# First modulation: half of its weight blocks through TensorE in float32, the other half on VectorE, and the scaled input split in two steps

## The chip, the core and the metric

The kernel runs on one core of a Trainium2 chip. The core has a matrix engine (TensorE, in the profile PE for matmuls and PEld for weight loads), three other compute engines (VectorE: DVE; ScalarE: ACT; GpSimd: POOL), an engine that issues the DMAs here (SyncE: SP), and 16 DMA engines that bring data from HBM into the on-chip memory (SBUF). Matmul results go to a second on-chip memory (PSUM), of 8 banks with 512 float32 columns on 128 partitions. The metric is the device time of one execution in microseconds; lower is better.

## The reference, cut to what matters

Six network stages run one after the other on a sequence of 512 tokens of width 1024. The change is at the very front of the first. There a condition vector `c` of 1024 numbers gives, by a matrix product with `w_ada`, a scale and a shift for each of the 1024 features:

```python
cond = jax.nn.silu(c)
mod = cond @ w_ada[l] + b_ada[l]                    # (1024) @ (1024 x 6144)
sh_m, sc_m, g_m, sh_f, sc_f, g_f = jnp.split(mod[:, None, :], 6, axis=-1)
h = layer_norm(x) * (1.0 + sc_m) + sh_m             # 512 x 1024
mix = hybrid_mixer(h, w_in[l], ...)                 # starts with h @ w_in
```

In the kernel `1 + sc_m` is G and `sh_m` is B; each needs 1024 x 1024 numbers of `w_ada`. Everything later waits for `h`.

## The kernel before, in words

Nearly all matmuls are float32 products built of three products in a reduced format: each operand is split into a high part (`hh`, `wh`) and the rest (`hl`, `wl`), and `mm3` (L116 to L120) issues high x high, low x high and high x low. A weight block is loaded by SP into one of five `wr` buffers, rounded into `wh` by ScalarE (L101), and the rest `wl` is taken by VectorE (L102). The first user of `h` is `dt_project` (a block of 48 columns), then come the projections of `proj_in`, each of 128 columns.

The head of the kernel is this. `cond_cols` makes `silu(c)` as a 128 x 8 tile: column k holds the 128 values of feature block k. `mix_load` loads X and normalises it (L306, L772, `rsqrt`, L776). `gemv_cols` runs twice, for G and for B. Each run has two halves of 512 columns, and each half four loads of 512 KB, 16 loads in all, numbered 1 to 16 here: 1 to 4 for G's first half, 5 to 8 for its second, 9 to 12 and 13 to 16 for B. A load brings two weight blocks of 128 x 512, one for an even k, `r[:, 0]`, and one for an odd k, `r[:, 1]`.

Every block is multiplied by its `cond` column, one number for each partition, and added up. The even blocks go through VectorE into `acc[0]` (L200, L202). The odd ones go into `acc[1]`: GpSimd multiplies the first (L200), ScalarE scales the second and third in place (L204) and GpSimd adds them (L205), and VectorE adds the last (L202). Then TensorE sums over the 128 partitions: each 128-column slice of an `acc` is the stationary operand and a column of ones the moving one (L209, eight float32 matmuls for a half, of which the trace shows two records each). VectorE takes the four columns from PSUM into G or B (L211). All four halves write into one PSUM tile, `sums`, one bank.

`mix_hT` transposes X on TensorE (L787), into four tiles of the pool `pa` and four of `pb`. For each of the eight feature blocks ScalarE then forms `h = X*G + B` (L791) and its high part (L792), and VectorE the low part (L793). One `pb` tile is `sums`, so the eighth block's transposes wait until another `pb` tile is free.

The program's text doesn't set the order of the instructions: a scheduler places them, each engine runs its list strictly in that order, and semaphores carry the waits between engines. A `wr` buffer is loaded anew when all that read it are done.

Of the kernel before, what the change touches and what calls it, by code (L numbers as in the profile page):

```python
# [7 lines left out]
F32 = mybir.dt.float32  # L8
F32R = mybir.dt.float32r
I32 = mybir.dt.int32  # L10
AF = mybir.ActivationFunctionType
OP = mybir.AluOpType
# [6 lines left out]
KD = 8  # L19
# [14 lines left out]
def blk(c):  # L34
    return slice(128 * c, 128 * c + 128)


class Kern:
# [148 lines left out]
    def gemv_cols(self, cond, w, n0, bcol, add, dst, p):  # L187


        nc = self.nc  # L190
        for h in range(2):
            c0 = n0 + 512 * h
            acc = [self.t(), self.t()]
            for k2 in range(4):
                r = self.wrp.tile([128, 2, 512], F32, name="wr", tag="wr")
                nc.sync.dma_start(r, w[k2 * 256:k2 * 256 + 256, c0:c0 + 512].rearrange("(k p) n -> p k n", p=128))
                for j, eng in enumerate((nc.vector, nc.gpsimd)):
                    k = 2 * k2 + j
                    if k2 == 0:
                        eng.tensor_scalar(acc[j], r[:, j], cond[:, k:k + 1], None, op0=OP.mult)  # L200
                    elif j == 0 or k2 == 3:
                        nc.vector.scalar_tensor_tensor(acc[j], r[:, j], cond[:, k:k + 1], acc[j], op0=OP.mult, op1=OP.add)  # L202
                    else:
                        nc.scalar.activation(r[:, j], r[:, j], AF.Copy, scale=cond[:, k:k + 1])  # L204
                        eng.tensor_add(acc[j], acc[j], r[:, j])  # L205
            cs = slice(4 * h, 4 * h + 4)
            for j in range(4):
                for i in range(2):
                    nc.tensor.matmul(p[:, 4 * h + j:4 * h + j + 1], acc[i][:, blk(j)], self.ones[:, 0:1],  # L209
                                     start=(i == 0), stop=(i == 1))  # L210
            nc.vector.scalar_tensor_tensor(dst[:, cs], p[:, cs], add, bcol[:, cs], op0=OP.add, op1=OP.add)  # L211

    def gemv(self, ends, cond, w, bcol, n0, kind, dst, scale=1.0, bias=0.0):
# [565 lines left out]
    def mix_hT(self, X, G, B):  # L779

        nc = self.nc
        self.new_hT()
        P = []
        for k in range(KD):
            p = self.pa() if k < 4 else self.pb()
            for t in range(NT):
                nc.tensor.transpose(p[:, blk(t)], X[:, t, blk(k)], self.ident)  # L787
            P.append(p)
        for k in range(KD):
            h = self.t()  # L790
            nc.scalar.activation(h, P[k], AF.Identity, bias=B[:, k:k + 1], scale=G[:, k:k + 1])  # L791
            nc.scalar.activation(self.hh[:, k], h, AF.Copy)  # L792
            nc.vector.tensor_sub(self.hl[:, k], h, self.hh[:, k].bitcast(F32))  # L793

    def mix_cols(self, V4):
        io, V = self.io, self.nc.vector
# [1641 lines left out]
```

## Time and profile before

| | us |
|---|---|
| median of 3 runs | 2830.43 (2826.44 to 2836.71) |
| the profiled execution's own time | 2836.87 |
| span, from its first to its last instruction | 2835.1 |
| TensorE busy | 2543.7, 90% of the span |
| VectorE, ScalarE, GpSimd busy | 1940.3, 1289.9, 757.9 |
| first projection's first matmul (L118) | at 44.61 |

All rows come from one execution. A timeline row has the start, the time from the start of the first to the end of the last instruction of the row, engine, line, operation, tile written <- tiles read, shapes, count, and in brackets how long the engine had been idle and what ended that. Ends of matmuls are modelled, so the distance between two starts is the better measure of a matmul. A float32 matmul has two records.

### The profile page before, as it was taken

The page shows a single profiled execution, that of the slowest core. Times are in us where ns is not written, and L with a number is a line of the kernel's source. Part 1 is how long each engine was busy: PE and PEld are TensorE (multiplying, and loading weights), DVE is VectorE, ACT ScalarE, POOL GpSimd, SP SyncE. Part 2 cuts the span into 40 slices and gives each one's busy share as a digit, 9 for nine tenths or more (in the row PEclk, how much of TensorE's full clock was granted, in tenths as well). Part 3 has the DMA queues.
Part 4 walks back from the last instruction along what each step waited for, and adds up shares of the span by engine and source line. Part 5 has one row for each costly group of instructions (what it writes and reads, how often), then busy time and mean ns, then how long its engine had stood idle before and what let it go on. Part 6 is the DMA issues. An engine that isn't in the chain of part 4 may idle for free.

```text
span 2835.1 us, 35075 instructions
## 1 busy us (share of the span) xinstructions
PE 2543.7 (90%) x12272; PEld 2072.8 (73%) x12272; DVE 1940.3 (68%) x3253; ACT 1289.9 (45%) x2138; POOL 757.9 (27%) x597
## 2 busy tenths in 40 slices
PE   6889899799999998798995898889999889899997
PEld 5777687578878776676774676767777777788885
DVE  7667678665667657679998877777767676843436
ACT  3444455533555433467774544453333435432412
POOL 2224333420122220321213213325345422500002
PEclk8999999899999897899997988999999989999998
DMA  7333244334454674689986243234444556433331
GB/s 224 87 92 99 74 119 117 85 87 126 142 172 139 197 246 145 217 279 341 362 311 160 82 127 114 77 116 130 138 140 129 159 198 197 123 108 97 97 97 60
DMA packets 382014, 425.95 MB, mean 150 GB/s; under 512 B 35447, under 2 KB 249578, under 8 KB 381834
## 3 DMA queue, kind: packets, MB, share of 16 engines
q1 hardware_dynamic: 375322, 401.11, 45.6%
q0 software_dynamic: 5936, 20.48, 2.3%
q8 instruction: 97, 1.59, 0.2%
q10 hardware_dynamic: 576, 2.10, 0.2%
q14 instruction: 83, 0.68, 0.1%
HBM read 389.14 MB, written 32.11 MB: 149 GB/s over the span
## 4 chain that ended last, share of the span: by engine, by line
PE 40%; DVE 11%; DMA 5%; ACT 4%; issue 3%; POOL 2%; SPq 0%; POOLq 0%; ACTq 0%; DVEq 0%
PE pb L119 8%; PE pb L118 8%; PE pb L120 8%; PE pa L118 5%; PE pa L119 5%; PE pa L120 4%; DVE wl L102 3%; ACT wh L101 1%; PE pa L954 1%; DVE m L102 1%; DVE X L336 1%; DMA wr<-in_mod_mix_w 1%; DVE xl L102 1%; DMA wr<-in_mlp_w 1%; DMA wr<-dT 1%
## 5 line engine op out<-in xcount | busy, mean ns | idle before, releaser
L102 DVE TENSOR_TENSOR wl<-wr,wh 128x1024 fp32r<-128x1024 f32 (+3 forms) x486 | 620.4, 1287 | 469.8 <-ACT wh L101 464.1
L101 ACT ACTIVATE wh<-wr 128x1024 fp32r<-128x1024 f32 (+3 forms) x486 | 493.7, 1026 | 686.5 <-PE pa L119 289.1
L118 PE MATMUL pa<-hh,wh 128*128 128x512 f32 (+1 forms) x1240 | 500.2, 404 | 15.6 <-ACT m L1283 7.6
L119 PE MATMUL pa<-hl,wh 128*128 128x512 f32 (+1 forms) x1240 | 492.2, 397 | 0.0
L120 PE MATMUL pa<-hh,wl 128*128 128x512 f32 (+1 forms) x1240 | 490.6, 396 | 0.0
L118 PEld LDWEIGHTS pa<-hh,wh 128*128 128x128 f32 (+1 forms) x1240 | 238.0, 192 | 68.8 <-ACT wh L101 9.4
L234 POOL TENSOR_TENSOR ga<-ga,wr 128x512 f32<-128x512 f32 x96 | 136.8, 1425 | 538.7 <-DVE ga L230 252.6
L120 PEld LDWEIGHTS pa<-hh,wl 128*128 128x128 f32 (+1 forms) x1240 | 236.8, 191 | 51.6 <-issue 0.5
L119 PEld LDWEIGHTS pa<-hl,wh 128*128 128x128 f32 (+1 forms) x1240 | 238.0, 192 | 47.7 <-issue 0.5
L118 PE MATMUL pb<-wh,m 128*128 128x512 f32 x520 | 207.7, 403 | 20.2 <-DVE t L335 14.6
L119 PE MATMUL pb<-wl,m 128*128 128x512 f32 x520 | 208.7, 401 | 2.2 <-DVE wl L102 2.2
L120 PE MATMUL pb<-wh,m 128*128 128x512 f32 x520 | 205.5, 400 | 0.0
L101 ACT ACTIVATE m<-t 128x512 fp32r<-128x512 f32 (+1 forms) x168 | 101.3, 608 | 151.5 <-DVE t L723 92.3
L102 DVE TENSOR_TENSOR m<-t,m 128x512 fp32r<-128x512 f32 (+1 forms) x168 | 135.2, 812 | 49.1 <-ACT m L101 46.3
L118 PE MATMUL pb<-m 128*128 128x256 f32 (+7 forms) x440 | 151.3, 351 | 18.0 <-ACT m L101 17.9
L674 POOL TENSOR_TENSOR wr<-wr,gate 128x512 f32<-128x512 f32 x40 | 62.6, 1589 | 345.4 <-DMA wr<-in_mlp_w 290.5
L119 PE MATMUL pb<-m 128*128 128x256 f32 (+7 forms) x440 | 146.8, 334 | 6.3 <-DVE m L102 6.3
L120 PE MATMUL pb<-m 128*128 128x256 f32 (+7 forms) x440 | 143.6, 329 | 0.0
L118 PEld LDWEIGHTS pb<-wh,m 128*128 128x128 f32 x520 | 99.4, 191 | 46.6 <-DVE t L335 12.4
L230 DVE SCALAR_TENSOR_TENSOR ga<-wr,cs,ga 128x512 f32<-128x512 f32 x128 | 100.6, 788 | 45.0 <-POOL ga L234 39.9
L232 ACT ACTIVATE wr<-wr,cs 128x512 f32<-128x512 f32 x96 | 69.3, 722 | 126.2 <-DMA wr<-in_mod_ffn_w 47.4
L118 PE MATMUL pa<-m,wh 128*128 128x512 f32 x248 | 106.8, 435 | 20.1 <-ACT m L101 6.9
(715 smaller groups left out, 5408.2 us busy)
## 6 DMA issues: line engine op xcount, KB each, us to landing
wr<-in_mlp_w SPq DMA_DIRECT2D x128, 512.0 KB
wr<-in_w_in SPq DMA_DIRECT2D x96, 512.0 KB
wr<-in_w_exp_up SPq DMA_DIRECT2D x64, 512.0 KB
wr<-in_w_exp_gate SPq DMA_DIRECT2D x64, 512.0 KB
wr<-in_w_exp_down SPq DMA_DIRECT2D x64, 512.0 KB
wr<-in_w_ada SPq DMA_DIRECT2D x48, 512.0 KB
wr<-in_mod_mix_w SPq DMA_DIRECT2D x48, 512.0 KB
wr<-in_mod_ffn_w SPq DMA_DIRECT2D x48, 512.0 KB
```

Source lines behind the costliest of these rows:

```text
L101: self.after(self.nc.scalar.activation(hi, src, AF.Copy), first)
L102: self.nc.vector.tensor_sub(lo, src, hi.bitcast(F32))
L118: mm(out, lh, rh, start=st, stop=False)
L119: mm(out, lh, rl, start=False, stop=False)
L120: mm(out, ll, rh, start=False, stop=sp)
L230: nc.vector.scalar_tensor_tensor(acc, r[:, j], cond[:, k:k + 1], acc, op0=OP.mult, op1=OP.add)
L232: nc.scalar.activation(r[:, j] if k else acc, r[:, j], AF.Copy, scale=cond[:, k:k + 1])
L234: nc.gpsimd.tensor_add(acc, acc, r[:, j])
L336: nc.vector.tensor_add(self.X[:, t, c], self.X[:, t, c], tp)
L674: self.nc.gpsimd.tensor_mul(r[:, j], r[:, j], gate[:, 512 * h:512 * h + 512])
L954: self.nc.tensor.transpose(p[:, 128 * c:128 * c + 128], src[:, 128 * c:128 * c + 128], self.ident)
```

## The change

Two things are changed. In `gemv_cols` the blocks of even k no longer go through VectorE: each is the stationary operand of four float32 matmuls with the `cond` column as the moving one (L204 of the new file), which multiply and sum at once and add up in PSUM. The odd blocks all go through VectorE into the one `acc` (L200, L202), and four matmuls with ones (L206) add its sum over partitions. ScalarE and GpSimd have no part in it. In `mix_hT` X is first multiplied by G alone, on VectorE in place in PSUM for blocks 0 to 3 (L789) and on ScalarE into SBUF for 4 to 7 (L792). B is added as the high and the low part are formed (L795 on ScalarE, L796 on VectorE).

```diff
@@ gemv_cols
-            acc = [self.t(), self.t()]
+            acc = self.t()
+            into = lambda i: p[:, 4 * h + i:4 * h + i + 1]
             for k2 in range(4):
                 r = self.wrp.tile([128, 2, 512], F32, name="wr", tag="wr")
                 nc.sync.dma_start(r, w[k2 * 256:k2 * 256 + 256, c0:c0 + 512].rearrange("(k p) n -> p k n", p=128))
-                for j, eng in enumerate((nc.vector, nc.gpsimd)):
-                    k = 2 * k2 + j
-                    if k2 == 0:
-                        eng.tensor_scalar(acc[j], r[:, j], cond[:, k:k + 1], None, op0=OP.mult)
-                    elif j == 0 or k2 == 3:
-                        nc.vector.scalar_tensor_tensor(acc[j], r[:, j], cond[:, k:k + 1], acc[j], op0=OP.mult, op1=OP.add)
-                    else:
-                        nc.scalar.activation(r[:, j], r[:, j], AF.Copy, scale=cond[:, k:k + 1])
-                        eng.tensor_add(acc[j], acc[j], r[:, j])
+                k = 2 * k2
+                if k2 == 0:
+                    nc.vector.tensor_scalar(acc, r[:, 1], cond[:, k + 1:k + 2], None, op0=OP.mult)
+                else:
+                    nc.vector.scalar_tensor_tensor(acc, r[:, 1], cond[:, k + 1:k + 2], acc, op0=OP.mult, op1=OP.add)
+                for i in range(4):
+                    nc.tensor.matmul(into(i), r[:, 0, blk(i)], cond[:, k:k + 1], start=k == 0 and i == 0, stop=False)
+            for i in range(4):
+                nc.tensor.matmul(into(i), acc[:, blk(i)], self.ones[:, 0:1], start=False, stop=i == 3)
             cs = slice(4 * h, 4 * h + 4)
-            for j in range(4):
-                for i in range(2):
-                    nc.tensor.matmul(p[:, 4 * h + j:4 * h + j + 1], acc[i][:, blk(j)], self.ones[:, 0:1],
-                                     start=(i == 0), stop=(i == 1))
@@ mix_hT
         for k in range(KD):
-            h = self.t()
-            nc.scalar.activation(h, P[k], AF.Identity, bias=B[:, k:k + 1], scale=G[:, k:k + 1])
-            nc.scalar.activation(self.hh[:, k], h, AF.Copy)
-            nc.vector.tensor_sub(self.hl[:, k], h, self.hh[:, k].bitcast(F32))
+            if k < 4:
+                nc.vector.tensor_scalar(P[k], P[k], G[:, k:k + 1], None, op0=OP.mult)
+            else:
+                h = self.t()
+                nc.scalar.activation(h, P[k], AF.Copy, scale=G[:, k:k + 1])
+                P[k] = h
+        for k in range(KD):
+            nc.scalar.activation(self.hh[:, k], P[k], AF.Identity, bias=B[:, k:k + 1])
+            nc.vector.scalar_tensor_tensor(self.hl[:, k], P[k], B[:, k:k + 1], self.hh[:, k].bitcast(F32), op0=OP.add,
+                                           op1=OP.subtract)
```

The scheduler's order shifts with it. Two places follow, on TensorE and on VectorE, with the semaphores that a row waits for in brackets.

On TensorE, the end of the modulation before: loads 13 to 16 appear only as the finished sums `t_269` and `t_270`, and the first projection (L118) follows.

```order
L209 MATMUL pb_181<-ones_88,t_269 128x1 [waits DVE_49]
L209 MATMUL pb_181<-ones_88,t_270 128x1 [waits DVE_49]
...
L118 MATMUL pa_412<-hh_298,wh_408 48x512 [waits PE_49,Activation_49]
L119 MATMUL pa_412<-hl_299,wh_408 48x512 [waits DVE_49]
L120 MATMUL pa_412<-hh_298,wl_409 48x512 [waits DVE_49]
```

The same place now. `wr_285`, `wr_292`, `wr_299` and `wr_306` are loads 13 to 16, `t_250` and `t_284` the VectorE sums of B's two halves, `pb_355` the eighth block of X.

```order
L206 MATMUL pb_181<-ones_88,t_250 128x1 [waits DVE_49]
...
L784 MATMUL pb_355<-ident_90,X_123 128x128 [waits Activation_49]
...
L204 MATMUL pb_181<-cs1_112,wr_285 128x1 [waits DMAHW7_49,DVE_49]
L204 MATMUL pb_181<-cs1_112,wr_285 128x1 x3
L204 MATMUL pb_181<-cs1_112,wr_292 128x1 [waits DMAHW0_49]
...
L204 MATMUL pb_181<-cs1_112,wr_306 128x1 [waits DMAHW2_49]
...
L206 MATMUL pb_181<-ones_88,t_284 128x1 x4
L118 MATMUL pa_428<-hh_318,wh_424 48x512 [waits DVE_49,Activation_49]
```

TensorE has 20 matmuls for the last half in place of 8. The first of them waits for VectorE as well as for its load (for which instruction, the next rows show), and the eighth block's transposes stand ahead of them instead of inside the first projection.

On VectorE, the same loads before (`pb_181` is `sums`, `B1_180` is B; `wr_271` to `wr_285` are loads 13 to 16):

```order
L200 TENSOR_SCALAR t_269<-wr_271,cs1_112 128x512 [waits DMAHW7_49]
L202 SCALAR_TENSOR_TENSOR t_269<-wr_275,cs1_112,t_269 128x512 [waits DMAHW0_49,DVE_49]
L202 SCALAR_TENSOR_TENSOR t_269<-wr_280,cs1_112,t_269 128x512 [waits DMAHW1_49,DVE_49]
L211 SCALAR_TENSOR_TENSOR B1_180<-pb_181,V4_120 128x4 [waits PE_49]
L202 SCALAR_TENSOR_TENSOR t_269<-wr_285,cs1_112,t_269 128x512 [waits DMAHW2_49,DVE_49]
L202 SCALAR_TENSOR_TENSOR t_270<-wr_285,cs1_112,t_270 128x512 [waits Pool_49]
```

And now:

```order
L200 TENSOR_SCALAR t_284<-wr_285,cs1_112 128x512 [waits DMAHW7_49]
L202 SCALAR_TENSOR_TENSOR t_284<-wr_292,cs1_112,t_284 128x512 [waits DMAHW0_49,DVE_49]
L202 SCALAR_TENSOR_TENSOR t_284<-wr_299,cs1_112,t_284 128x512 [waits DMAHW1_49,DVE_49]
L202 SCALAR_TENSOR_TENSOR t_284<-wr_306,cs1_112,t_284 128x512 [waits DMAHW2_49,DVE_49]
L208 SCALAR_TENSOR_TENSOR B1_180<-pb_181,V4_120 128x4 [waits PE_49]
L796 SCALAR_TENSOR_TENSOR hl_319<-pa_320,B1_180,hh_318 128x512 [waits Activation_49]
```

The instruction that takes the sums of loads 9 to 12 out of PSUM (L211 before, L208 now) stood ahead of the work on load 16 and now stands behind it. It is what the first L204 on `wr_285` waits for, since both touch the bank of `sums`. For G the same holds: its first L208 stands behind the work on loads 5 to 8.

On SP the order stays, but the waits of the loads change. A load into a used `wr` buffer waited for VectorE and GpSimd; it now waits for VectorE and TensorE, that is for the four L204 on the load that lay there before: load 10 for those on load 5, loads 11, 12 and 13 for those on 6, 7 and 8, loads 14, 15 and 16 for those on 9, 10 and 11, and the first full block of `w_in` for those on load 13.

Behind this head all work is the same, but the scheduler sets some of it in another order: of those whose names tell them apart, 462 TensorE and 313 VectorE instructions stand elsewhere among the rest, by at most 59 and 19 places.

## Rows read from the trace of the kernel before

**Rows 1.** The page: busy time by engine, and TensorE's granted clock in 40 slices.
```profile
PE 2543.7 (90%) x12272; PEld 2072.8 (73%) x12272; DVE 1940.3 (68%) x3253; ACT 1289.9 (45%) x2138; POOL 757.9 (27%) x597
...
PEclk8999999899999897899997988999999989999998
```
**Rows 2.** Waits of TensorE from 44 to 300 us: us in total, times, longest us.
```profile
PE pb L118 <- ACT m L101: 8.6, 3, 6.4
PE pa L118 <- ACT m L1283: 7.6, 2, 6.6
```
**Rows 3.** Timeline of TensorE: the first projections.
```profile
44.61 0.64 PE L118 MATMUL pa<-hh,wh 128*48 128x512 f32 x1
45.05 0.63 PE L119 MATMUL pa<-hl,wh 128*48 128x512 f32 x1
...
48.89 1.05 PE L787 MATMUL pb<-ident,X 128*128 128x128 f32 x4
49.60 0.76 PE L118 MATMUL pa<-hh,wh 128*128 128x512 f32 x1
...
50.89 0.39 PE L118 MATMUL pa<-hh,wh 128*128 128x512 f32 x1
51.11 0.39 PE L119 MATMUL pa<-hl,wh 128*128 128x512 f32 x1
```
**Rows 4.** Windows: each engine's busy us; then PEclk, DMA share and GB/s.
```profile
24.00:25.00 1.00, 0.78 (x7) 0.78 (x8) 1.00 (x3) 0.36 (x1) 0.00 (x0) 1.00 0.48 184
25.00:26.00 1.00, 1.00 (x12) 1.00 (x10) 1.00 (x4) 0.36 (x1) 0.51 (x1) 1.00 0.29 51
...
29.00:30.00 1.00, 0.71 (x5) 0.71 (x6) 1.00 (x3) 0.00 (x0) 1.00 (x1) 0.86 1.00 344
...
44.00:50.00 6.00, 6.00 (x19) 3.73 (x20) 5.07 (x9) 5.92 (x10) 0.00 (x0) 0.50 1.21 293
50.00:51.00 1.00, 1.00 (x5) 0.64 (x5) 1.00 (x2) 0.97 (x3) 0.00 (x0) 0.90 1.23 292
```
**Rows 5.** Timeline of all engines: sums of the modulation's halves, and B's last load.
```profile
25.81 1.62 PE L209 MATMUL pb<-ones,t 128*128 128x1 f32 x14
...
29.08 0.15 DVE L211 SCALAR_TENSOR_TENSOR G<-pb,V 128x4 f32<-128x4 f32 x1
...
29.29 3.20 PE L209 MATMUL pb<-ones,t 128*128 128x1 f32 x16 [1.86 <-DVE G L211]
...
39.77 1.78 DVE L202 SCALAR_TENSOR_TENSOR t<-wr,cs,t 128x512 f32<-128x512 f32 x2 [0.48 <-DMA wr<-in_w_ada]
...
40.94 3.81 PE L209 MATMUL pb<-ones,t 128*128 128x1 f32 x16 [2.05 <-DVE t L202]
```
**Rows 6.** Timeline of all engines: VectorE with and without GpSimd beside it.
```profile
14.28 0.74 DVE L202 SCALAR_TENSOR_TENSOR t<-wr,cs,t 128x512 f32<-128x512 f32 x1
...
14.87 1.27 POOL L205 TENSOR_TENSOR t<-t,wr 128x512 f32<-128x512 f32 x1 [1.26 <-ACT wr L204]
14.94 1.22 DVE L282 TENSOR_TENSOR rt<-ri 128x4 f32<-128x4 f32 x1
...
25.30 3.86 DVE L202 SCALAR_TENSOR_TENSOR t<-wr,cs,t 128x512 f32<-128x512 f32 x4
```
**Rows 7.** Timelines of SP and ACT: issues of loads 6 and 16, landing of 6.
```profile
17.59 0.37 SPq L196 DMA_DIRECT2D wr<-in_w_ada  x1
...
21.47 0.72 ACT L204 ACTIVATE wr<-wr,cs 128x512 f32<-128x512 f32 x1 [1.31 <-DMA wr<-in_w_ada]
...
34.50 0.37 SPq L196 DMA_DIRECT2D wr<-in_w_ada  x1
```
**Rows 8.** Lines L791 to L793: count, duration ns min/median/max, first and last start.
```profile
L791 ACT ACTIVATE t<-pa,B,G x4: 769/776/782, 39.3 to 41.3; 128x512 f32<-128x512 f32 x4
...
L792 ACT ACTIVATE hh<-t x8: 626/632/637, 42.0 to 50.9; 128x512 fp32r<-128x512 f32 x8
...
L793 DVE TENSOR_TENSOR hl<-t,hh x8: 678/688/692, 42.7 to 51.6; 128x512 fp32r<-128x512 f32 x8
```

## The prediction

> **What bounds the kernel now.** I read the page first: TensorE is busy for 90% of the span, at the full granted clock or near it in most slices [rows 1]. So time is lost where TensorE starves or runs at the lower clock. The waits of TensorE come next: from 44 to 300 us the longest single one is 6.6 us, and the two largest groups make 16.2 us together [rows 2]. Behind the head the first stage is a stream of matmuls; the other engines follow it. A microsecond by which that stream starts later is then a microsecond at the end, and only the first 50 us need working out.
>
> Third, the timelines of the head. The first projection's matmul starts at 44.61 [rows 3]. Just before it come sixteen records of L209, from 40.94 [rows 5]: these wait for VectorE's last two additions, and those for load 16, which lands at 39.77 [rows 5]. So the chain is load 16, two additions, eight matmuls, stream: 44.61 - 39.77 = 4.84 us from landing to stream. Fourth, the clock: 1.0 (2.4 GHz) until it falls in the window 29 to 30 to a mean of 0.86, so at about 29.7, then 0.50 (1.2 GHz) until about 50.1 [rows 4]. In between TensorE does L209 in three bursts, and it is 5.5 us into the stream when the clock rises. One float32 matmul of this kind (two records) takes 2 x 1.62/14 = 0.23 us at 2.4 GHz and 2 x 3.20/16 = 0.40 us at 1.2 GHz [rows 5]. A projection matmul takes 0.44 us at 1.2 GHz and 0.22 at 2.4, by the distance of starts [rows 3].
>
> **What goes.** VectorE's tail loses one of two additions, some 0.75 us without GpSimd beside it [rows 6]; ScalarE's and GpSimd's parts go altogether. GpSimd had slowed VectorE: a 128x4 operation took 1.22 us beside one of its additions, and four additions took 3.86 us where one alone takes 0.74 [rows 6]. The Trainium skill (SBUF — State Buffer, section SBUF: two separate sides) has the two share a port pair, held by one for a whole instruction; these rows agree. But VectorE's early lead buys little, as the loads bound it: loads 6 to 8 wait for the landing of loads 4 and 5, which the change doesn't touch. The traffic behind them sinks to 184 and 51 GB/s at 24 to 26 us [rows 4], so load 8 is in by about 25.
>
> The eighth block's transposes leave the stream: 49.60 - 48.89 = 0.7 us [rows 3]. In the second half of `mix_hT` ScalarE has one operation after B in place of two, 0.63 to 0.78 us for 1.41 [rows 8]. That is hidden on both sides: TensorE has 12 dt matmuls and 9 of the next projection to do, 9 us at 1.2 GHz, before it needs block 4. Should the clock be 2.4 GHz there, that cover is 4.7 us, and the high and low parts behind the new tail, 0.7 us each [rows 8], come late by some 0.5 us; that goes into a rival. The four L789 on VectorE (PSUM in and out) stand in no row before. Bounds: the 0.74 of an addition and ScalarE's 0.78 from PSUM [rows 6, 8], 3 us in all, beside a wait for load 10 that is longer.
>
> **What comes: TensorE as a consumer of loads.** Each load now costs TensorE four matmuls, and each half four more: 20 x 0.40 = 8.0 us at 1.2 GHz, 4.6 at 2.4. The 16 of a half can't start before VectorE has taken the half before out of the one PSUM bank. The trace has that wait already: sixteen L209 records sat 1.86 us for the G operation at 29.08 [rows 5]. There it held no buffer. Now it does, since a `wr` buffer is released by the L204 behind the wait.
>
> The sum, with 0.75 us for each addition, and 21.4 - 17.6 = 3.8 us from issue to landing (load 6, with little else under way [rows 7]; load 16 took 39.8 - 34.5 = 5.3 us in a full queue [rows 5, 7]). I take 3.8, since the loads are now spaced by TensorE:
>
> - Load 8 at 25, two additions, L208 of G's first half at 26.2. G's second half on TensorE from 26.4: fourteen matmuls at 2.4 GHz, the others at 1.2, done at 30.1; the four sums at 31.7.
> - Load 10 waits for the first four: issue 27.3, landing 31.1, addition, and the next L208 behind it at 32.1.
> - B's first half on TensorE from 32.2: 16 x 0.40, at 38.6; sums 40.2. Loads 14, 15 and 16 wait for the matmuls on 9, 10 and 11: issue at 33.8, 35.4 and 37.0. Load 16 lands at 40.8 (before: 39.8).
> - Addition 41.6, L208 of B's first half 41.8, and only then B's second half: 41.9 + 8.0 = 49.9. The stream starts at 50.0.
>
> That is 5.4 us later than 44.6, less 0.7 for the transposes: **4.7 us**. The clock is taken to rise 5.5 us into the stream, as before. The blocks of `w_in` are late too: the first full one waits for the matmuls on load 13 (43.5), lands at 47.3 and is used behind the 12 dt matmuls, 12 x 0.44 us from 50.0 on, at 55.3; so they add nothing.
>
> Against the profiled execution (2836.87, span 2835.1) this is 2841.6; the median of the runs is 6.4 lower than that execution, so I put the 4.7 on the median, 2830.4: **2835.1 us**.
>
> **Rivals.**
>
> *The clock is at 2.4 GHz through the new tail.* TensorE has more to do from 26 us on, almost without a gap. Then: L208 of G's second half at 32.1 again (load 10 bounds it), B's first half 3.7 us to 35.9, load 16 issued at 35.0 and in at 38.8, the tail 39.8 + 4.6 = 44.4, stream at 44.5. Gains 0.1 and 0.7; and the about twelve matmuls that ran at 1.2 GHz in the stream run at 2.4, 12 x 0.22 = 2.6; less 0.5 for the late high and low parts: -2.9, 2827.5. Against it: the L209 bursts from 30 to 44.6 filled most of that time and the clock stayed at 0.50 [rows 4, 5], and L204 is the same shape.
>
> *The weight load doesn't follow the clock.* The 0.40 comes from bursts that started behind a wait [rows 5]; if L204, whose stationary operand is there early, kept the 0.23 us of 2.4 GHz also at 1.2, the stream would start at 44.5 as above, but at 1.2 GHz: -0.1 - 0.7, 2829.6. Against it: the sixteen records from 29.29 have no wait inside and still take 0.20 us each. The Trainium skill has this rule (TensorE: Matmul & The Clock Gate, section LDWEIGHTS (loading the stationary operand)): a weight load takes its columns divided by 1.2 GHz, 107 ns for 128, with no word of the granted clock. The trace is near that at 2.4 GHz (0.116 a record) and not at 1.2 (0.20).
>
> *Slower: the loads come late after their release.* With 5.3 us from issue to landing, as for load 16 in the full queue [rows 5, 7], load 10 lands at 32.6 and its L208 comes at 33.6; B's first half starts at 33.7, load 16 is issued at 38.5 and lands at 43.8, the tail runs from 44.9 to 52.9: 8.4 - 0.7 = +7.7. If the clock also falls at 26 instead of 29.7, TensorE ends G's second half at 34.4, load 16 lands at 44.7, and the stream starts at 53.9: +8.6, 2839.0. It turns slower by my bound when the stream starts at 53.8 or later. For it: load 16 did take this long. Against: the queue was full then because nothing held the loads back.
>
> *The later order decides.* Behind the head the work is the same in a slightly other order. The nearest price is the longest single wait of TensorE, 6.6 us [rows 2]: one more or one fewer, 2829 to 2842 with the 4.7. That the change doesn't do what it says is only this: the half on VectorE does get shorter, and the path doesn't run through it.
>
> **How the numbers follow.** My forecast 0.45, the higher clock 0.22, the load's price 0.05, late loads 0.18, the later order 0.10. About 0.3% (8.5 us: below 2822, above 2839) is what a measurement of this kernel can tell from no change. Faster: the higher clock with 5.6 us of luck in the later order, 0.22 x 0.18 = 0.04, and 0.02 for the rest. Slower: 0.18 x 0.6 = 0.11 for late loads, 0.04 for a forecast that is 4 us short, half of the last case, 0.05: 0.20. Same: 0.74. The range takes in the higher clock with 3 us of order below it (2824) and the late loads with 4 us above (2843).
>
> **What would show it.** In the profile after: L208 of B's first half starts about 1 us after load 16's landing, near 41.8, and sixteen L204 matmuls start right behind it; TensorE's waits in the head name L208; loads 10 and 14 to 16 are issued right after L204 matmuls; first L118 near 50 with PEclk 0.50 from about 30 to 55. If L118 starts before 46, the clock or the price of 0.40 was wrong; if load 16 lands after 43, the 3.8 was. If L118 is near 50 and the time still is below 2827, the later order gave it back.

## The result: slower by 0.94%, and the profile after

| | us |
|---|---|
| before, median of 8 runs | 2828.43 (2821.59 to 2836.71) |
| after, median of 8 runs | 2854.05 (2845.97 to 2860.0) |
| ratio, 95% interval | 1.0094, 1.008 to 1.0107 |
| profiled execution of after: own time, span | 2859.6, 2857.9 |

The change costs 25.6 us; 4.7 was forecast. In the profiled executions the spans differ by 22.8 us (2857.9 against 2835.1). Half of that is there when the stream starts, at 55.84 for 44.61 [rows 3]; the other half arises far behind the head.

The timeline of after in the head, SP, TensorE and VectorE (columns as in [rows 3]):

```profile
26.35 0.75 DVE L202 SCALAR_TENSOR_TENSOR t<-wr,cs,t 128x512 f32<-128x512 f32 x1 [0.57 <-DMA wr<-in_w_ada]
27.02 0.15 DVE L208 SCALAR_TENSOR_TENSOR G<-pb,V 128x4 f32<-128x4 f32 x1
27.23 6.99 PE L204 MATMUL pb<-cs,wr 128*128 128x1 f32 x32 [1.85 <-DVE G L208]
29.13 12.73 SPq L197 DMA_DIRECT2D wr<-in_w_ada  x7
...
34.08 1.84 PE L206 MATMUL pb<-ones,t 128*128 128x1 f32 x8
35.96 0.16 DVE L208 SCALAR_TENSOR_TENSOR G<-pb,V 128x4 f32<-128x4 f32 x1 [2.39 <-PE pb L206]
...
36.18 6.99 PE L204 MATMUL pb<-cs,wr 128*128 128x1 f32 x32 [0.26 <-DVE G L208]
...
43.02 1.85 PE L206 MATMUL pb<-ones,t 128*128 128x1 f32 x8
...
44.73 1.09 PE L784 MATMUL pb<-ident,X 128*128 128x128 f32 x4
46.41 0.75 DVE L202 SCALAR_TENSOR_TENSOR t<-wr,cs,t 128x512 f32<-128x512 f32 x1 [1.10 <-DMA wr<-in_w_ada]
47.08 0.15 DVE L208 SCALAR_TENSOR_TENSOR B<-pb,V 128x4 f32<-128x4 f32 x1
47.29 6.99 PE L204 MATMUL pb<-cs,wr 128*128 128x1 f32 x32 [1.46 <-DVE B L208]
...
54.14 1.84 PE L206 MATMUL pb<-ones,t 128*128 128x1 f32 x8
55.84 0.64 PE L118 MATMUL pa<-hh,wh 128*48 128x512 f32 x1
```

From 27.23 to 55.84 TensorE works with short waits alone (0.26 and 1.46 us): three halves of 6.85 us from the first L204 to the first L206 (0.43 us for each matmul of two records) and three bursts of sums of 1.8. The last of the seven loads is issued as late as 41.5 (the row of SP ends at 41.86), since each waits for the L204 on the load that lay in its buffer, and load 16 lands at 46.41.

The clock, in windows of after (busy us of the five engines; then PEclk, DMA share, GB/s):

```profile
10.00:20.00 10.00, 7.93 (x36) 7.71 (x37) 8.55 (x30) 0.23 (x1) 0.00 (x0) 1.00 0.93 297
...
26.00:27.00 1.00, 0.00 (x0) 0.00 (x0) 0.65 (x1) 0.00 (x0) 0.00 (x0) 0.84 0.15 57
27.00:28.00 1.00, 0.77 (x4) 0.77 (x4) 0.96 (x4) 0.00 (x0) 0.00 (x0) 0.50 0.01 4
...
60.00:61.00 1.00, 1.00 (x4) 0.60 (x3) 1.00 (x3) 1.00 (x2) 0.00 (x0) 0.59 1.19 294
```

It falls in TensorE's wait before 27.23, at 26.7 by the mean of that window, not at 29.7 [rows 4], and rises at 60.8, 5.0 us into the stream (before: at 50.2, 5.6 us into it).

Behind the head, the waits of TensorE in the expert stage, 1165 to 1225 us, of after and then of an experiment with nearly the same head but before's order (sums_only, below); us in total, times, longest:

```profile
PE pb L120 <- DVE ael L1676: 10.1, 1, 10.1
```
```profile
PE pb L119 <- DVE wl L102: 4.0, 2, 3.4
...
PE pb L120 <- DVE ael L1669: 0.3, 1, 0.3
```

And VectorE there, after and then sums_only:

```profile
1190.41 0.21 DVE L1723 CAST tk<-twa 128x1 f32<-128x1 int32 x2 [9.60 <-DMA twa<-TW]
1190.54 1.22 DVE L102 TENSOR_TENSOR wl<-wr,wh 128x1024 fp32r<-128x1024 f32 x1
1191.67 0.68 DVE L1676 SCALAR_TENSOR_TENSOR ael<-pa,aeh 128x512 fp32r<-128x512 f32 x1
```
```profile
1182.36 2.35 DVE L102 TENSOR_TENSOR wl<-wr,wh 128x1024 fp32r<-128x1024 f32 x2
1184.63 0.68 DVE L1669 SCALAR_TENSOR_TENSOR ael<-pa,aeh 128x512 fp32r<-128x512 f32 x1
1191.33 0.21 DVE L1716 CAST tk<-twa 128x1 f32<-128x1 int32 x2 [6.02 <-DMA twa<-TW]
```

The two casts (L1723 in after, L1716 in sums_only) wait for a table that a DMA reads back. The scheduler has put them ahead of `ael`, which the first expert's TensorE work needs; VectorE works through its list in order, so TensorE waits with them. In sums_only `ael` stands ahead of the casts, and behind them comes `wl`, for which TensorE waits 3.4 us there.

A second place is the attention stage. Three rows of TensorE mark it, with equally many TensorE instructions left in both kernels at each: one ahead of the expert stage, the wait that opens the attention stage, and the first row behind that stage (L1893 in after, L1886 in sums_only). After, then sums_only:

```profile
1150.23 0.61 PE L1493 MATMUL pb<-r_both,r_tri 128*128 128x16 f32 x2 [6.92 <-DVE r_both L1484]
...
1555.47 0.91 PE L344 MATMUL pa<-ident,X 128*128 128x128 f32 x3 [13.06 <-ACT X L324]
...
1829.14 0.24 PE L1893 MATMUL pa<-ident,t 32*128 32x32 f32 x1
```
```profile
1150.37 0.61 PE L1486 MATMUL pb<-r_both,r_tri 128*128 128x16 f32 x2 [6.91 <-DVE r_both L1477]
...
1546.63 0.69 PE L344 MATMUL pa<-ident,X 128*128 128x128 f32 x2 [14.40 <-ACT X L324]
...
1814.10 0.25 PE L1886 MATMUL pa<-ident,t 32*128 32x32 f32 x1
```

The attention stage takes 273.7 us in after and 267.5 in sums_only. At the stream's start after is 0.6 us behind sums_only, at 1150 level with it, at the opening of the attention stage 8.8 behind, at its end 15.0 and at the program's end 19.8 (spans 2857.9 and 2838.1). So 9.0 us arise from the expert stage to the attention stage, 6.2 in the attention stage and 4.8 behind it; the last were not followed up. By all their runs, though, the two kernels are only 11 us apart (0.39%, next table). These two executions show where the order loses, and how much only roughly.

### The profile page after: what moved, and what is told of

Same layout as the page of the kernel before. It is cut to its first block, busy times and chain, and to the rows that moved or that the text cites. A ratio compares the mean times of both kernels' runs of the same rounds, so it can differ in the third digit from the quotient of the medians.

```text
span 2857.9 us, 35227 instructions
## 1 busy us (share of the span) xinstructions
PE 2568.5 (90%) x12368; PEld 2098.2 (73%) x12368; DVE 1934.3 (68%) x3253; ACT 1281.9 (45%) x2126; POOL 734.8 (26%) x585
## 4 chain that ended last, share of the span: by engine, by line
PE 40%; DVE 11%; DMA 6%; ACT 4%; issue 3%; POOL 2%; SPq 0%; POOLq 0%; ACTq 0%; DVEq 0%
PE pb L118 8%; PE pb L119 8%; PE pb L120 7%; PE pa L118 5%; PE pa L119 4%; PE pa L120 4%; DVE wl L102 3%; ACT wh L101 2%; PE pa L958 1%; DVE m L102 1%; DMA wr<-in_mlp_w 1%; DMA wr<-in_w_exp_gate 1%; DMA wr<-dT 1%; DVE ga L227 1%; DVE t L332 1%
## 5 line engine op out<-in xcount | busy, mean ns | idle before, releaser
L101 ACT ACTIVATE wh<-wr 128x1024 fp32r<-128x1024 f32 (+3 forms) x486 | 493.7, 1026 | 692.7 <-PE pa L119 274.0
L118 PE MATMUL pa<-hh,wh 128*128 128x512 f32 (+1 forms) x1240 | 498.6, 402 | 15.4 <-ACT m L1287 6.5
L118 PEld LDWEIGHTS pa<-hh,wh 128*128 128x128 f32 (+1 forms) x1240 | 237.6, 192 | 68.1 <-ACT wh L101 10.3
L118 PE MATMUL pb<-wh,m 128*128 128x512 f32 x520 | 207.6, 403 | 20.5 <-DVE t L332 14.7
L118 PE MATMUL pb<-m 128*128 128x256 f32 (+7 forms) x440 | 150.8, 350 | 17.2 <-ACT m L101 16.9
L118 PEld LDWEIGHTS pb<-wh,m 128*128 128x128 f32 x520 | 99.4, 192 | 47.1 <-DVE t L332 12.9
L119 PE MATMUL pb<-wl,xh 128*128 128x512 f32 x256 | 105.5, 412 | 19.6 <-DVE wl L102 19.5
```

The lines of the kernel that those rows point to most:

```text
L101: self.after(self.nc.scalar.activation(hi, src, AF.Copy), first)
L118: mm(out, lh, rh, start=st, stop=False)
L119: mm(out, lh, rl, start=False, stop=False)
```

## The experiments

The table gives the ratio to before with its 95% interval, and from the one profile of each: the first L118, TensorE's wait for the first `ael`, VectorE's idle time ahead of the two casts, and the length of the attention stage between the last two of the three rows just shown. "Order" is that behind the head.

| kernel | order | ratio | L118 at | `ael` | casts | attention |
|---|---|---|---|---|---|---|
| before | before's | 1 | 44.61 | 0.3 | 11.7 | 270.4 |
| after | after's | 1.0094 (1.008 to 1.0107) | 55.84 | 10.1 | 9.6 | 273.7 |
| sums_only | before's | 1.0055 (1.0032 to 1.0078) | 55.29 | 0.3 | 6.0 | 267.5 |
| scale_only | close to before's | 1.001 (0.9994 to 1.0026) | 47.72 | 0.3 | 0 | 266.5 |
| two_banks | before's | 1.0059 (1.0035 to 1.0082) | 53.23 | 0.3 | 5.1 | 267.7 |
| quarter | another | 1.0031 (1.0014 to 1.0048) | 44.62 | 0.3 | 1.4 | 270.3 |
| null_t1 | before's | 1.0003 (0.9988 to 1.0018) | 45.24 | 0.3 | 0 | 268.5 |
| order_t3 | close to after's | 1.0026 (1.0012 to 1.004) | 44.87 | 4.1 | 4.4 | 274.8 |
| order_t5 | another | 1.0014 (0.9997 to 1.0031) | 46.80 | 0.3 | 11.5 | 271.1 |
| pace | close to after's | 1.0088 (1.0067 to 1.0109) | 55.20 | 8.1 | 7.6 | 275.0 |
| casts_first | before's, casts moved | 1.0022 (1.0003 to 1.004) | 44.28 | 12.4 | 11.7 | 265.6 |
| casts_late_before | before's, casts moved | 1.0 (0.9982 to 1.0019) | 45.50 | 0.3 | 0 | 267.4 |
| casts_late_after | after's, casts moved | 1.0058 (1.0037 to 1.0079) | 53.62 | 0.3 | 0 | 275.7 |
| casts_late_t3 | as order_t3, casts moved | 1.0027 (1.0012 to 1.0043) | 45.62 | 0.3 | 0 | 274.0 |

**sums_only** and **scale_only**: the changed `gemv_cols` with the old `mix_hT`, and the reverse (the diff of either is the half of the change that the name says).

> The change to gemv_cols alone; the scaling of X as before. Behind the head the scheduler puts all instructions in the very order of the kernel before, where in the changed kernel they stand in another. If half of the loss lies in that other order, this kernel has a stream that starts as late as that of the changed one (first L118 at 55 to 57 us, 11 to 12 later than before's 44.61) and the time is before's plus these 11 to 12 us: 2838 to 2842, ratio 1.004. If instead a late stream costs twice its lateness whatever the order (late loads and buffers collide with the stages behind), it is 20 to 26 us slower, ratio 1.007 to 1.009, like the changed kernel.

> The change to mix_hT alone; the modulation's sums as before. The chain behind load 16 has one ScalarE operation (0.77 us) less, so the stream should start 0.5 to 1 us earlier than 44.61. The order behind the head differs from before's in a few places only (late in the program, some 52 TensorE instructions). If the order matters only where it is much changed, 2826 to 2831, ratio 0.999 to 1.001. If the new scaling by itself brings the order that costs 10 us, ratio 1.003 to 1.004.

sums_only is 15.5 us slower by the ratio's 0.55%, its stream 10.7 us late: the first answer rather than the second, though the interval (9 to 22 us) is wide. scale_only shows no change, as expected, but its stream came 3.1 us later instead of earlier: VectorE, which still shares the additions with GpSimd there, has the four scalings (L789 in after) on top, 2.7 us from 31.18, and load 16's addition starts at 43.91. That reason is read from the rows and was not tried.

**two_banks**: each half of 512 columns has its own bank.

```diff
-            into = lambda i: p[:, 4 * h + i:4 * h + i + 1]
+            into = lambda i: p[h][:, i:i + 1]
...
-            sums = K.pb()
+            sums = [K.pb(), K.pb()]
```

> The changed kernel with the sums of first and second halves in two PSUM banks, so that L204 of a half no longer waits for VectorE to take the half before out. If TensorE's own time is what makes the stream late (L204 at 0.43 us, 6.99 us a half, L206 1.84), only the waits go, 0.74 + 1.85 + 0.26 + 1.46 us at most: stream at 52 to 54. If the wait on the bank is the cause, through the buffers that it holds, the stream starts at 46 to 49. The order behind the head is nearly that of scale_only: if the order of the changed kernel costs the other half, the time is before's plus 8 to 10 us, 2836 to 2839; if lateness costs double, 2843 to 2848.

Its TensorE timeline:

```profile
26.46 5.26 PE L204 MATMUL pb<-cs,wr 128*128 128x1 f32 x24
31.58 1.85 PE L206 MATMUL pb<-ones,t 128*128 128x1 f32 x8
33.29 6.96 PE L204 MATMUL pb<-cs,wr 128*128 128x1 f32 x32
40.11 1.84 PE L206 MATMUL pb<-ones,t 128*128 128x1 f32 x8
41.82 6.97 PE L204 MATMUL pb<-cs,wr 128*128 128x1 f32 x32
48.65 1.84 PE L206 MATMUL pb<-ones,t 128*128 128x1 f32 x8
...
53.23 0.78 PE L118 MATMUL pa<-hh,wh 128*48 128x512 f32 x1
```

No row has a wait, and the stream still starts at 53.23. So the wait on the bank costs about 2.6 us, and TensorE's own time the rest. The ratio lies between the two expectations.

**quarter**: the second and fourth load of each half go through VectorE whole.

```diff
+                if k2 % 2:
+                    nc.vector.scalar_tensor_tensor(acc, r[:, 0], cond[:, k:k + 1], acc, op0=OP.mult, op1=OP.add)
+                    continue
                 for i in range(4):
                     nc.tensor.matmul(into(i), r[:, 0, blk(i)], cond[:, k:k + 1], start=k == 0 and i == 0, stop=False)
```

> The changed kernel with only half as many blocks on TensorE (those of the first and third load of each half); the second and fourth load go through VectorE whole. TensorE has 32 float32 matmuls of 0.43 us less, 13.7 us. If TensorE's time is the cause, the loads bound the head again: load 16 lands at 40 to 43 and the stream starts at 44.5 to 47. If the wait on the bank is the cause, it stays at 50 or later, since each half still waits for the L208 of the half before. Time by the first: before's plus 0 to 3 us and whatever its own later order costs.

```profile
39.48 3.57 PE L207 MATMUL pb<-cs,wr 128*128 128x1 f32 x16 [2.23 <-DVE B L211]
42.92 1.84 PE L209 MATMUL pb<-ones,t 128*128 128x1 f32 x8
44.62 0.64 PE L118 MATMUL pa<-hh,wh 128*48 128x512 f32 x1
```

The stream is back at 44.62 with the wait on the bank still there: TensorE's time was the main cause. Yet the kernel is 0.31% slower than before with an equally early stream.

**null_t1, order_t3, order_t5**: the kernel before, with one, three or five small VectorE instructions in `mix_hT`.

```diff
+        for _ in range(3):
+            nc.vector.tensor_scalar(B[:, 0:4], B[:, 0:4], 0.0, None, op0=OP.add)
```

> The kernel before with one more VectorE instruction in mix_hT, which adds 0.0 to four columns of B (under 0.2 us). The scheduler leaves everything behind the head in the order of before. It is the control for the next two: all theories expect no change, 2825 to 2831, ratio 1.000 within 0.002, first L118 at 44.5 to 46.

> The kernel before with three such VectorE instructions (under 0.5 us in the head). The scheduler answers with another order behind the head, one that is close to that of the changed kernel (69 TensorE instructions stand elsewhere against it, 333 against before). The stream starts as early as before's. If the order of the changed kernel costs some 10 us by itself, this kernel is 6 to 14 us slower than before, 2834 to 2842, ratio 1.002 to 1.005. If the loss behind the head is the price of a late stream, whatever the order, the time is that of the control, ratio 1.000 within 0.002.

> The kernel before with five such VectorE instructions (under 0.8 us). The order behind the head is close to that of quarter, which was 8.8 us slower than before with a stream as early as before's. If that loss was the order's, this kernel is 5 to 12 us slower, ratio 1.002 to 1.004; if it was something in quarter's head that its first L118 does not show, ratio 1.000 within 0.002.

With one such instruction nothing changes. With three, the head stays (44.87), the order behind it becomes nearly that of after, and the kernel loses 0.26% (7.4 us; interval 3.4 to 11.3): an order costs by itself, without any late stream. Its attention stage takes 274.8 us, between these rows:

```profile
1529.99 0.69 PE L347 MATMUL pa<-ident,X 128*128 128x128 f32 x2 [14.87 <-ACT X L327]
...
1804.75 0.25 PE L1891 MATMUL pa<-ident,t 32*128 32x32 f32 x1
```

order_t5 stays open: its interval holds 0 and 8.8 us alike. Nor did it get quarter's order: compared by their tiles in the traces, some 190 TensorE instructions stand elsewhere in the two, about as many as between before and quarter (45 between order_t3 and after). So what quarter loses is not settled.

**pace**: after, with a transpose of the same block into a spare bank behind each L204.

```diff
                     nc.tensor.matmul(into(i), r[:, 0, blk(i)], cond[:, k:k + 1], start=k == 0 and i == 0, stop=False)
+                    nc.tensor.transpose(self.spare[:, blk(i)], r[:, 0, blk(i)], self.ident)
```

> The changed kernel with a transpose of the same weight block into a spare PSUM bank added behind each L204: 64 records with 128 moving columns, whose results nothing reads. At the records' distance of 0.21 us they add 13.7 us to TensorE's work in the head, at 0.11 us 7.1. If the distance in the head is 0.21 us whatever TensorE does there (so that the price of L204 is fixed), the stream starts at 66 to 70 us and the time is 22 us or more above before. If matmuls with more columns bring the higher rate and hold it, a half costs 3.6 + 1.8 + 0.9 = 6.3 us instead of 8.8, the loads bound the head, and the stream starts at 45 to 50, earlier than the changed kernel's 55.8 although TensorE does more.

Neither came: the stream starts at 55.20, as in after, with 64 more records. The scheduler placed many of the transposes in bursts, and the rows (timeline of TensorE, then windows) show the clock rise behind them and fall under the L204 that follow:

```profile
37.25 1.06 PE L205 MATMUL pb<-ident,wr 128*128 128x128 f32 x4
...
38.53 1.06 PE L205 MATMUL pb<-ident,wr 128*128 128x128 f32 x4
39.39 3.07 PE L204 MATMUL pb<-cs,wr 128*128 128x1 f32 x26
42.32 0.31 PE L205 MATMUL pb<-ident,wr 128*128 128x128 f32 x1
```
```profile
36.00:38.00 2.00, 2.00 (x11) 2.00 (x10) 1.49 (x3) 0.66 (x1) 0.00 (x0) 0.50 0.97 364
...
40.00:42.00 2.00, 2.00 (x20) 2.00 (x20) 0.00 (x0) 0.00 (x0) 0.00 (x0) 1.00 0.29 30
42.00:44.00 2.00, 2.00 (x18) 2.00 (x17) 0.00 (x0) 0.00 (x0) 0.00 (x0) 0.75 0.86 321
44.00:46.00 2.00, 2.00 (x11) 2.00 (x11) 0.75 (x1) 0.00 (x0) 0.00 (x0) 0.50 0.86 272
```

From 39.39 to 42.32, nearly all of it at 2.4 GHz, thirteen L204 (26 records) take 2.93 us, 0.23 each; at 1.2 GHz they take 0.43. What the higher clock gives, the transposes take.

**casts_first, casts_late_before, casts_late_after, casts_late_t3**: the two casts ahead of the first `ael` (in the kernel before), and held back behind the third (in before, in after, in order_t3). `self.after` makes its first argument wait for its second; `self.low` lists the `ael` instructions.

```diff
@@ casts_first: moe_actT (the casts are issued at the stage's start)
+        for tok in self.toks:
+            self.after(low, tok)
@@ the other three: moe_hots
-            self.nc.vector.tensor_copy(tok, self.tw[:, e, 0:1].bitcast(I32))
+            self.after(self.nc.vector.tensor_copy(tok, self.tw[:, e, 0:1].bitcast(I32)), self.low[2])
```

> The kernel before with one thing moved behind the head: the two casts of the expert stage that read twa (they wait for a table that a DMA reads back, and their results are used only at the end of the stage) stand ahead of the first ael on VectorE instead of right behind it. That is the place which the changed kernel's scheduler gave them; everything else keeps the order of before. If this place is where the changed order loses, TensorE waits 4 to 10 us for the first ael (0.3 in null_t1), and the time is 2 to 8 us above before: ratio 1.001 to 1.003 (the casts already hold up the next low parts in some executions of before, so not the whole wait is new). If the loss is elsewhere in the order, ratio 1.000 within 0.001.

> The kernel before with the same two casts held back until behind the third ael, some 30 us later, when the table has long landed; all else in the order of before. VectorE's idle time ahead of these casts was 0 to 11.7 us in the profiles of kernels with this order (11.7 in that of before, 0 in null_t1, 5 to 6 in sums_only and two_banks). If it sits on the path, the time falls by its mean, 2 to 6 us: 2821 to 2825, ratio 0.998 to 0.9993. If something else waits for the same table then, ratio 1.000.

> The changed kernel with the two casts held back in the same way; its head and nearly all of its order stay (72 TensorE and 5 VectorE instructions move). If the 10.1 us that TensorE waits for the first ael is the order's price, the time falls by 6 to 10 us, to 2844 to 2848, ratio to before 1.006 to 1.0075 in place of 1.0094, and about the 11 us of the late stream stay, with 5 from other places. If the order costs elsewhere, it stays at 1.009.

> order_t3 (before's head, nearly the changed kernel's order, ratio 1.0026) with the two casts held back. If they are the whole price of that order, the ratio comes to that of casts_late_before, 0.998 to 1.000. If half of the price is elsewhere (the profile shows TensorE waiting 6.1 us for hl at 1783 us where kernels with before's order wait 4.1, and 5.5 for the softmax), 1.0005 to 1.0015.

casts_first has the wait of after, and before's stream and attention stage (TensorE's waits, 1150 to 1200 us):

```profile
PE pb L120 <- DVE ael L1672: 12.4, 1, 12.4
```

It costs 0.22%, 6 us (interval 1 to 11). In after, holding the casts back takes that wait away (0.3 us) and the ratio from 1.0094 to 1.0058, 10 us; the intervals just part, so this is known to some 7 us either way, and the stream of its one profile starts 2.2 us earlier as well. In before and in order_t3 it changes nothing that can be measured. That is not because nothing waits at the casts there: in the profile of before, where `ael` stands ahead of them, TensorE waits for the `wl` behind them instead (1150 to 1215 us):

```profile
PE pb L119 <- DVE wl L102: 9.1, 1, 9.1
```

In null_t1, with the same order, the casts had nothing to wait for. So the column `ael` alone is not what after's order adds at this place, and a wait in one profile is not the mean of the runs. Of order_t3's price no part could be shown to be the casts'; of its places the attention stage is the one that stands out. casts_late_before is no faster than before, so no version here beats it.

## Why the prediction was wrong

Its direction and its mechanism in the head hold; two steps failed, one in the head and one behind it. Of the 20.9 us by which the forecast was short, 5.8 lie in the head (the stream at 55.84 for 50.0). The others lie behind it, where the step "only the first 50 us need working out" had put nothing.

*The step that failed first* is the one that put fourteen of G's second-half matmuls at 2.4 GHz, with the clock falling at 29.7 as in before. TensorE waits 1.85 us for L208 just there, the clock falls in that wait, and the half takes 6.85 us, not 3.7. By terms, forecast 50.0 against 55.84: load 8 and the start of the half 0.8 later; its matmuls 3.2 longer, the sums 0.3, less 0.4 of slack, as load 10 was to bound that L208; so it starts at 35.96 for 32.1. Load 16 is issued 4.5 later and took 4.9 us from issue (41.5) to landing for 3.8, so that L208 of B comes at 47.08 for 41.8. The tail took 8.55 for 8.0, as the price was 0.43 and not 0.40. The prediction's own sign for the 3.8, a landing after 43, was thus ambiguous: 1.1 us of the 5.6 by which load 16 was late are that term, the others the matmuls ahead of it. Two slips in the recorded sum (25 and two additions of 0.75 make 26.5, not 26.2; fourteen matmuls of 0.23 and two of 0.40 from 26.4 on end at 30.4, not 30.1) are worth some 0.4 us, since load 10 was to bound the next step.

*The price of 0.40* was read from the burst at 29.29, and that burst straddles the fall at 29.7: its first four records stand 0.11 us apart, the other twelve 0.21. So it was 7% low. That a weight load might keep its time at any clock was rightly set aside: the records stand 0.11 us apart at the higher clock and 0.21 at the lower. The Trainium skill (TensorE: Matmul & The Clock Gate, section LDWEIGHTS (loading the stationary operand)) gives a weight load its columns divided by 1.2 GHz, by estimate 107 ns for 128; a record took 0.214 us here at 1.2 GHz, so the trace does not agree there.

*The wait of each half on the L208 of the half before* was right in place and order: each first L204 names L208, and L208 of B starts 0.67 us behind load 16's landing. The prediction gave that wait no price of its own; two_banks shows about 2.6 us for it, and quarter that the rest is the matmuls.

*The 0.7 us of the eighth block's transposes* left the stream as forecast; they stand in TensorE's wait at 44.73. The high and low parts of blocks 4 to 7 and the late `w_in` blocks were costed at nothing, and rightly: some 60 us into the stream, where before transposes `m` (L954, at 105.09), after comes 10.2 us later (L958, at 115.25) and sums_only 10.5 (L951, at 115.62), no more than at the stream's start (11.2 and 10.7). sums_only and two_banks, 15.5 and 16.7 us slower with streams 10.7 and 8.6 late, still leave 5 to 8 us over, which is about the half-width of their intervals. It was not settled.

*The rival "late loads"* gave the stream's start best: 53.9 with the clock falling at 26; it fell at 26.7. *The rival "the later order decides"* was the second failure. I priced it by the longest single wait between 44 and 300 us, 6.6 us, either way, and half of a tenth went to slower. By the runs of after and sums_only, whose streams start 0.6 us apart, after's order costs 0.39%, 11 us (roughly 3 to 19).

Two places of it stand out. One is the attention stage: 273.7 to 275.7 us in the five profiles with that order or nearly it, 274.6 on average; 265.6 to 271.1 in the nine others, 268.3 on average; so 6.3 us. The other is the two casts, 10 us in after. The first is carried by order_t3 and by the profiles, the second by casts_late_after and, more weakly, casts_first. Which instruction of the attention stage makes its 6.3 us was not tried; TensorE is idle there for 44.5 us in after and 39.5 in sums_only, of which it waits 14.9 us for the softmax tile `t` in after, and 11.3 for `t` and `se` in sums_only.

The three together, 11.2 for the stream, 6.3 and 10, make 27.5; the measured 25.6 has an interval of 22.6 to 30.3. But the two prices of the order make 16.3 where the runs of after and sums_only give 11. That a late stream and another order both cost is shown; how the order's part divides is not.

## What to carry to other kernels

Work that is moved to TensorE as one-column matmuls has to be priced at the clock that TensorE will have there: look at the distance of records in that very stretch, on one side of a change of the clock, and count the whole sum against the time of the loads; here three halves of 8.6 to 8.7 us filled a head that the loads had bounded before. Where a scheduler sets the order, an edit of under 0.5 us at the front can change the order of instructions 2000 us and more behind it (order_t3); compare the two orders for waiting instructions (here two casts behind a DMA) that have come ahead of urgent ones, over the whole program and not its first tenth.

## What was not expected of the hardware

The column of the granted clock says 1.00 in the first 26 us of after, but TensorE does not keep the pace of 2.4 GHz there. Its timeline:

```profile
12.51 7.02 PE L204 MATMUL pb<-cs,wr 128*128 128x1 f32 x32 [0.74 <-DVE ra L266]
19.38 0.88 PE L784 MATMUL pa<-ident,X 128*128 128x128 f32 x3
```

The 32 records of G's first half stand 6.87/32 = 0.215 us apart, the distance that L204 has at 0.50; only from 23.26 on is it 0.11. In two_banks all L204 shown above keep that distance too, while the column has, in a window among them:

```profile
30.00:40.00 10.00, 10.00 (x49) 10.00 (x48) 4.58 (x8) 0.00 (x0) 0.00 (x0) 1.00 0.74 235
```

So ahead of the first change that the column shows, the distance between starts tells the pace, and not the column. In that kernel 24 us of L204 and L206 without a gap (26.46 to 50.35) kept the distance of 0.21; in pace the column's rises at 39.6 and 49.8 came right behind runs of transposes.
